# Alternating the halves of TensorE's array in four places of a one-core hybrid decoder step

## The chip, the cores and the metric

One core of a Trainium2 chip runs the whole program in one launch. The metric is the device time of one execution in microseconds (us). The kernel before was run three times: 764.14, 760.05 and 762.81 us, median 762.81.

## The reference

304 rows of 1024 numbers (16 learned rows and 256 prompt rows, and 8 sample sequences of 4 rows) go through one layer:

```
p = rmsnorm(x) @ w_in                       # columns for 4 GLA heads and for 8 RWKV-7 heads
GLA:   lg = log_sigmoid(gl @ gate_w2 + b)/16; chunked attention with decay; states
RWKV:  w, a, g by low-rank matmuls; S = S*w - (S kk)(kk a) + v k; y = S r; states
x = x + concat(norm(o_gla)*silu(gg), (norm(y)+bonus)*gate) @ w_out
x = x + moe(rmsnorm(x))                     # top 1 of 4 groups, top 2 of 8 experts, 32 SwiGLU experts
y = rmsnorm(x)
```

It returns both outputs, the GLA and RWKV states of the prompt and of the samples, and the shift rows.

## The kernel before

All of it is float32. The input projection makes 26 column tiles of 128 (tile 14 is only 32 wide where it is used here, the GLA gate columns), each as a sum over eight pieces `k` of the 1024 inputs. The rows are kept transposed, so that a matmul streams 304 columns (`T`). For most tiles the weights and the inputs are split into high and low parts (`uh`, `ul`, `xh`, `xl`) and three products are summed; for tile 14 the weights are whole (`pieces[14]`) and two products per `k` are summed, each on a group of 32 of the array's columns, with group `k % 4` (line 494 and after). The four groups are summed later by the matrix that makes `lg` (tile `ps_lg`).

The RWKV heads lie in pairs: pair `p` (0 to 3) has its two heads in partitions 0 to 63 and 64 to 127, called `q` 0 and 1. For every chunk of 64 rows of the prompt (four, and the samples as a fifth, `sct`) and every head a 64x128 matmul makes the scores (`score`, `ps_sc`, `ps_sct`); VectorE masks them into `Sc`, ScalarE and GpSimd copy the diagonal blocks into `Dm`, and a VectorE loop of 31 passes over `Lt`, the transposed `Dm`, inverts all triangles at once (`job_inverse`, tiles `tmp`, `X`). Beside that loop VectorE makes the GLA operands: `mn` and `bT` from `ps_lg`, `qT` and `kT` from the projection. `job_level` makes the six levels of GLA's decayed scores (`E`, `F`, `ps_lev`) into `AT`; `job_gla_out(q)` makes `ps_o`, `ps_omps_o` (the norm's sums) and `oG`. `job_chain` runs the five RWKV chunks one after the other (`ps_G`, `GV`, `UV`, `ps_Y`, `YT`, `ps_S`, `state`). `job_rwkv_samples` makes the eight sample states of a pair with two 128x64 matmuls of 512 columns (`ps_fs`), `job_rwkv_state` the prompt's state (`ps_fp`, 16 small matmuls). Then come the output projection (`job_oproj`, `ps_op`, 16 groups), the router, and 32 experts whose weights SyncE loads into rooms of 512 KB, or halves of 256 KB, as these come free.

Nobody writes the order of the instructions by hand. Each `job_...` is a generator that hands its operations to `Flow` (all are recorded through line 356), and `Flow` picks the next one by a price per operation, a due time (`RANK`) and its own model of what is ready. So an edit in one job can move the work of others on every engine. `bank(name, least)` takes a PSUM bank; `least` is the number that must be free.

Of the kernel before, what the change touches and what calls it, by code (L numbers as in the profile page):

```python
# [361 lines left out]
def tile_step(ctx: ExitStack, tc: tile.TileContext, io):  # L362
# [127 lines left out]
    def job_project(tiles):  # L490
        for j in tiles:
            o = yield from bank(f"ps_in{j}", 2 if j < 14 else 1)
            for k in range(KT):
                yield from after(f"x{k}", f"u{j}_{k // 4}")
                if j == 14:

                    g = 32 * (k % 4)
                    for i, x in enumerate((xh, xl)):
                        PE.matmul(o[g:g + 32, :T], pieces[14][:, k * P:k * P + 32], x[:, k, :].bitcast(F32),
                                  start=(k < 4 and i == 0), stop=(k >= 4 and i == 1))  # L500
                else:
                    kk, (hi, lo) = slice(k % 4 * P, k % 4 * P + P), units[j, k // 4]
                    for i, (w, x) in enumerate(((hi, xh), (hi, xl), (lo, xh))):
                        PE.matmul(o[:, :T], w[:, kk], x[:, k, :], start=(k + i == 0), stop=(k == KT - 1 and i == 2))
                if k % 4 == 3:
                    mark(f"p{j}_{k // 4}")
                yield
# [210 lines left out]
    def job_scores():  # L718

        for p in range(4):  # L720
# [6 lines left out]
            Sc, Dm = late["Sc"], late["Dm"]  # L727
            for q in range(2):
                o = yield from bank(f"ps_sc{p}{q}")
                for c in range(4):  # L730
                    score(o[:, c * P:(c + 1) * P], p, q, c)
                V.tensor_tensor(Sc[q][:, 0:4, p, :], o.rearrange("p (c t) -> p c t", c=4),
                                sm.unsqueeze(1).to_broadcast([P, 4, P]), ALU.mult)
                flow.release(o)
# [5 lines left out]
        for q in range(2):  # L740
            o = yield from bank(f"ps_sct{q}")
            for p in range(4):
                score(o[:, p * P:(p + 1) * P], p, q, 4)
            late[f"sct{q}"] = o
# [295 lines left out]
    def job_rwkv_samples():  # L1040
# [23 lines left out]
        for p in range(4):  # L1064
            mb = t5((6, 1)[p % 2], f"UVb{p}", [P, 2, NS, 64])
            ob = yield from bank(f"ps_fs{p}", 2)
            for q in range(2):
                r = halves(q)[0]
                V.tensor_tensor(mb[:, q], us[q][:, 64 * p:64 * p + 64].unsqueeze(1).to_broadcast([P, NS, 64]),
                                seg[:, 1:9].unsqueeze(2).to_broadcast([P, NS, 64]), ALU.mult)  # L1070
                PE.matmul(ob[r, :], BKt[:, q, p, :], mb[:, q].rearrange("p b i -> p (b i)"), start=True, stop=True)
# [10 lines left out]
    def job_rwkv_state():  # L1082
# [7 lines left out]
        for p in range(4):  # L1090
            for q in range(2):
                r = halves(q)[0]
                PE.matmul(o[r, 64 * p:64 * p + 64], BKt[:, q, p, :], m[q][:, 64 * p:64 * p + 64], start=True, stop=False)
                PE.matmul(o[r, 64 * p:64 * p + 64], ident[r, 64 * q:64 * q + 64], state[r, p, :], start=False, stop=True)
# [1381 lines left out]
```

## Time and profile before

| | us |
|---|---|
| median of three runs | 762.81 |
| the profiled execution | 768.22 |
| span of its profile | 766.4 |
| mixer with its projections, to the output projection's start | 241.0 |
| output projection and router, to the first experts' start | 241 to 297 |
| experts and end | 297 to 766 |

The profiled execution took 5.41 us more than the median. A row of the timeline is the start and the length in us, the engine, the line, and the operation with what it writes and reads; for TensorE the numbers before the tile's size are the rows and columns of the array that it uses, and the profile has two records for one float32 matmul (`x8` is four matmuls). A bracket at the end is the idle time before it and what ended it. In a window's row each engine has its busy time and its records; the three numbers at the end are the granted TensorE clock as a share of 2.4 GHz, the DMA engines' busy share and GB/s.

### The profile page before, as it was taken

What the parts mean: (1) busy time and instruction counts of PE and PEld (TensorE: products, weight loads), DVE (VectorE), ACT (ScalarE), POOL (GpSimd) and SP (SyncE); (2) the same over time, 40 slices, a digit from 0 to 9 for tenths busy, and PEclk for the clock granted to TensorE, in tenths of its full rate; (3) what the DMA queues carried; (4) which work ended last, traced back from release to release, by engine and by line L of the source; (5) the groups of instructions that cost most, each with busy time, mean ns of one, the idle gap of its engine ahead of it and who ended that gap; (6) DMA issues with size and microseconds to landing.
All of it is one profiled execution on the core that took longest, in us unless ns stands there. A gap on an engine that the chain in (4) does not pass through costs nothing.

```text
span 766.4 us, 12595 instructions
## 1 busy us (share of the span) xinstructions
PE 689.2 (90%) x4610; PEld 353.0 (46%) x4610; DVE 306.1 (40%) x619; ACT 212.4 (28%) x525; POOL 138.2 (18%) x211
## 2 busy tenths in 40 slices
PE   6989997989998989999899999999989988988893
PEld 6878677878656975442223424323222221211131
DVE  6688479874576759521022312201111111101023
ACT  6887462554224431221011201111011010000003
POOL 3277325584352100400000000000010000000000
PEclk9989789889998987999999999999999999999998
DMA  8421115114267794999999999999999999999971
GB/s 308 139 83 56 56 50 200 57 57 170 99 242 239 265 328 173 410 416 415 418 418 417 418 419 418 419 416 416 419 415 415 418 417 414 415 410 414 414 297 69
DMA packets 66581, 230.63 MB, mean 301 GB/s; under 512 B 7920, under 2 KB 8944, under 8 KB 66000
## 3 DMA queue, kind: packets, MB, share of 16 engines
q1 hardware_dynamic: 65936, 229.45, 76.2%
q8 instruction: 38, 0.62, 0.3%
q10 hardware_dynamic: 576, 0.31, 0.2%
q14 instruction: 31, 0.25, 0.1%
HBM read 226.06 MB, written 3.67 MB: 300 GB/s over the span
## 4 chain that ended last, share of the span: by engine, by line


## 5 line engine op out<-in xcount | busy, mean ns | idle before, releaser
L356 PE MATMUL ps_in<-xh,uh 128*128 128x304 f32 x160 | 53.5, 335 | 6.6 <-ACT uh L356 6.6
L356 PE MATMUL ps_in<-xh,ul 128*128 128x304 f32 x160 | 53.8, 336 | 0.0
L356 PE MATMUL ps_in<-xl,uh 128*128 128x304 f32 x160 | 53.1, 332 | 0.0
L356 ACT ACTIVATE room_y<-ps_y,sw 128x512 fp32r<-128x512 f32 x18 | 11.7, 685 | 144.0 <-PE ps_sc L356 81.6
L356 DVE TENSOR_TENSOR room_AT<-room_AT,ps_sc 128x512 f32<-128x512 f32 x8 | 5.5, 687 | 110.7 <-PE ps_sc L356 110.7
L356 POOL TENSOR_TENSOR room_xl<-cst,prm 128x512 f32<-128x512 f32 x2 | 2.0, 1042 | 246.3 <-PE ps_y L356 246.3
L356 POOL TENSOR_TENSOR ul<-win,uh 128x512 fp32r<-128x512 f32 x28 | 37.2, 1331 | 32.5 <-ACT uh L356 28.8
L356 DVE TENSOR_TENSOR room_xg<-room_xg,ps_sc 48x512 f32<-48x512 f32 x16 | 10.6, 674 | 81.0 <-PE ps_sc L356 81.0
L356 PE MATMUL ps_xg<-oh,hl 128*128 128x256 f32 (+5 forms) x192 | 41.8, 345 | 0.9 <-DVE oh L356 0.9
L356 PEld LDWEIGHTS ps_in<-xh,uh 128*128 128x128 f32 x160 | 33.4, 209 | 8.4 <-ACT uh L356 6.6
L356 PEld LDWEIGHTS ps_xg<-oh,hl 128*128 128x128 f32 (+1 forms) x192 | 29.7, 198 | 16.5 <-issue 9.1
L356 PEld LDWEIGHTS ps_in<-xl,uh 128*128 128x128 f32 x160 | 33.4, 209 | 1.5 <-issue 1.0
L356 PEld LDWEIGHTS ps_in<-xh,ul 128*128 128x128 f32 x160 | 33.2, 207 | 1.4 <-issue 0.6
L356 PE MATMUL ps_h_w<-room_w,room_w 128*32 128x512 f32 (+1 forms) x104 | 28.6, 600 | 2.3 <-DMA room_w<-in_w 2.3
L356 ACT CAST ohT<-ps_ot 128x304 fp32r<-128x304 f32 x9 | 3.7, 413 | 95.1 <-PE ps_ot L356 95.0
L356 PE MATMUL ps_sc<-room_y,ohT 128*128 128x512 f32 (+1 forms) x96 | 28.0, 413 | 0.0
L356 ACT CAST uh<-win 128x512 fp32r<-128x512 f32 x40 | 24.4, 614 | 11.8 <-PE ps_in L356 11.6
L356 PE MATMUL ps_h_w<-Sc,room_w 128*64 128x512 f32 (+1 forms) x56 | 24.4, 602 | 0.3 <-DMA Sc<-in_w 0.2
L356 DVE SCALAR_TENSOR_TENSOR room_y<-ps_y,sw,room_y 128x512 fp32r<-128x512 f32 x18 | 12.9, 739 | 29.5 <-ACT room_y L356 29.3
L356 PE MATMUL ps_in<-xh,u 128*128 128x304 f32 x96 | 22.5, 313 | 0.6 <-DVE rx L356 0.6
L356 PEld LDWEIGHTS ps_sc<-room_y,ohT 128*128 128x128 f32 (+1 forms) x96 | 14.1, 166 | 17.3 <-issue 12.5
L356 PE MATMUL ps_h_w<-room_w,BKa 128*32 128x512 f32 x52 | 18.5, 603 | 1.5 <-DMA room_w<-in_w 1.5
(734 smaller groups left out, 1634.8 us busy)
## 6 DMA issues: line engine op xcount, KB each, us to landing
room_w<-in_w SPq DMA_DIRECT2D x99, 512.0 KB, 9.9
Sc<-in_w SPq DMA_DIRECT2D x53, 512.0 KB, 9.8
room_win<-in_w SPq DMA_DIRECT2D x48, 512.0 KB, 9.9
room_o<-in_w SPq DMA_DIRECT2D x31, 512.0 KB, 10.0
room_xh<-in_w SPq DMA_DIRECT2D x30, 512.0 KB, 9.9
UV<-in_w SPq DMA_DIRECT2D x29, 512.0 KB, 9.9
win<-in_win SPq DMA_DIRECT2D x27, 512.0 KB, 3.2
room_xl<-in_w SPq DMA_DIRECT2D x26, 512.0 KB, 10.0
```

The source lines that it names most:

```text
L356: lambda: method(*args, **kw)))
```

## The change

Four edits. The gate columns are issued eight at a time, when `k` is 3 and 7: four column groups with `xh`, then the four with `xl`. The scores of a pair take both banks first and alternate between `q` 0 and 1; both masks follow; the samples' scores alternate as well. The sample states make both masked operands on VectorE first and then issue both matmuls. The prompt state issues its eight `BKa` products first and then its eight products with the identity (`cst`); the accumulation starts with the first and stops with the last.

```diff
@@ -494,10 +494,10 @@
                 yield from after(f"x{k}", f"u{j}_{k // 4}")
                 if j == 14:
 
-                    g = 32 * (k % 4)
-                    for i, x in enumerate((xh, xl)):
-                        PE.matmul(o[g:g + 32, :T], pieces[14][:, k * P:k * P + 32], x[:, k, :].bitcast(F32),
-                                  start=(k < 4 and i == 0), stop=(k >= 4 and i == 1))
+                    for kk, x in [(kk, x) for x in (xh, xl) for kk in range(k - 3, k + 1)] if k % 4 == 3 else []:
+                        g = 32 * (kk % 4)
+                        PE.matmul(o[g:g + 32, :T], pieces[14][:, kk * P:kk * P + 32], x[:, kk, :].bitcast(F32),
+                                  start=(kk < 4 and x is xh), stop=(kk >= 4 and x is xl))
                 else:
                     kk, (hi, lo) = slice(k % 4 * P, k % 4 * P + P), units[j, k // 4]
                     for i, (w, x) in enumerate(((hi, xh), (hi, xl), (lo, xh))):
@@ -725,23 +725,25 @@
                 flow.give(late["Dm"])
                 G.memset(late["Dm"], 0.0)
             Sc, Dm = late["Sc"], late["Dm"]
+
+            os_ = [(yield from bank(f"ps_sc{p}0", 2)), (yield from bank(f"ps_sc{p}1"))]
+            for c in range(4):
+                for q in range(2):
+                    score(os_[q][:, c * P:(c + 1) * P], p, q, c)
             for q in range(2):
-                o = yield from bank(f"ps_sc{p}{q}")
-                for c in range(4):
-                    score(o[:, c * P:(c + 1) * P], p, q, c)
-                V.tensor_tensor(Sc[q][:, 0:4, p, :], o.rearrange("p (c t) -> p c t", c=4),
+                V.tensor_tensor(Sc[q][:, 0:4, p, :], os_[q].rearrange("p (c t) -> p c t", c=4),
                                 sm.unsqueeze(1).to_broadcast([P, 4, P]), ALU.mult)
-                flow.release(o)
+                flow.release(os_[q])
                 yield
             for q in range(2):
                 for h in range(2):
                     r = slice(64 * q + 32 * h, 64 * q + 32 * h + 32)
                     S.copy(Dm[r, :, p:16:4], Sc[q][r, 0:4, p, 32 * h:32 * h + 32].rearrange("p c t -> p t c"))
         for q in range(2):
-            o = yield from bank(f"ps_sct{q}")
-            for p in range(4):
-                score(o[:, p * P:(p + 1) * P], p, q, 4)
-            late[f"sct{q}"] = o
+            late[f"sct{q}"] = yield from bank(f"ps_sct{q}", 2 - q)
+        for p in range(4):
+            for q in range(2):
+                score(late[f"sct{q}"][:, p * P:(p + 1) * P], p, q, 4)
         yield
         for q in range(2):
             V.tensor_tensor(Sc[q][:, 4], late[f"sct{q}"].rearrange("p (x t) -> p x t", x=4),
@@ -1065,10 +1067,10 @@
             mb = t5((6, 1)[p % 2], f"UVb{p}", [P, 2, NS, 64])
             ob = yield from bank(f"ps_fs{p}", 2)
             for q in range(2):
-                r = halves(q)[0]
                 V.tensor_tensor(mb[:, q], us[q][:, 64 * p:64 * p + 64].unsqueeze(1).to_broadcast([P, NS, 64]),
                                 seg[:, 1:9].unsqueeze(2).to_broadcast([P, NS, 64]), ALU.mult)
-                PE.matmul(ob[r, :], BKt[:, q, p, :], mb[:, q].rearrange("p b i -> p (b i)"), start=True, stop=True)
+            for q in range(2):
+                PE.matmul(ob[halves(q)[0], :], BKt[:, q, p, :], mb[:, q].rearrange("p b i -> p (b i)"), start=True, stop=True)
             yield
             V.tensor_tensor(srw[:, p], ob.rearrange("p (b i) -> p b i", b=NS), srw[:, p], ALU.add)
             G.tensor_tensor(srw[:, p], srw[:, p], WLs[:, p, :].unsqueeze(2).to_broadcast([P, NS, 64]), ALU.mult)
@@ -1089,9 +1091,12 @@
             V.tensor_scalar(pairs(m[q][:, 0:256]), UV[:, q], seg[:, 0:1], None, op0=ALU.mult)
         for p in range(4):
             for q in range(2):
+                PE.matmul(o[halves(q)[0], 64 * p:64 * p + 64], BKt[:, q, p, :], m[q][:, 64 * p:64 * p + 64],
+                          start=(p == 0), stop=False)
+        for p in range(4):
+            for q in range(2):
                 r = halves(q)[0]
-                PE.matmul(o[r, 64 * p:64 * p + 64], BKt[:, q, p, :], m[q][:, 64 * p:64 * p + 64], start=True, stop=False)
-                PE.matmul(o[r, 64 * p:64 * p + 64], ident[r, 64 * q:64 * q + 64], state[r, p, :], start=False, stop=True)
+                PE.matmul(o[r, 64 * p:64 * p + 64], ident[r, 64 * q:64 * q + 64], state[r, p, :], start=False, stop=(p == 3))
         mark("uvs")
         yield
         fp = yield from t1("fp")
```

How the instructions move, at three places.

TensorE, scores of the last pair (`ps_sc30`, `ps_sc31`) and the gate columns (`ps_in14`), before:

```order
L356 MATMUL ps_in14_1018<-xl_108,win14_739 32x304
L356 MATMUL ps_sc30_1033<-AR_115,BK_116 128x128 x4
L356 MATMUL ps_b3_1032<-rx3_685,bl3_929 128x304
L356 MATMUL ps_in14_1018<-xh_107,win14_739 32x304
L356 MATMUL ps_sc31_1043<-AR_115,BK_116 128x128 x2
L356 MATMUL ps_g3_1047<-g2_740,lw_95 128x304
L356 MATMUL ps_sc31_1043<-AR_115,BK_116 128x128 x2
L356 MATMUL ps_in14_1018<-xl_108,win14_739 32x304
L356 MATMUL ps_in14_1018<-xh_107,win14_739 32x304
L356 MATMUL ps_in14_1018<-xl_108,win14_739 32x304
L356 MATMUL ps_in14_1018<-xh_107,win14_739 32x304
L356 MATMUL ps_in14_1018<-xl_108,win14_739 32x304
```

and with the change, from the first gate column on:

```order
L356 MATMUL ps_in14_1017<-xh_107,win14_736 32x304 x4
L356 MATMUL ps_in14_1017<-xl_108,win14_736 32x304 x4
L356 MATMUL ps_sc30_1036<-AR_115,BK_116 128x128
L356 MATMUL ps_sc31_1037<-AR_115,BK_116 128x128
L356 MATMUL ps_sc30_1036<-AR_115,BK_116 128x128
L356 MATMUL ps_sc31_1037<-AR_115,BK_116 128x128
L356 MATMUL ps_sc30_1036<-AR_115,BK_116 128x128
L356 MATMUL ps_sc31_1037<-AR_115,BK_116 128x128
L356 MATMUL ps_sc30_1036<-AR_115,BK_116 128x128
L356 MATMUL ps_sc31_1037<-AR_115,BK_116 128x128
L356 MATMUL ps_in14_1017<-xh_107,win14_736 32x304
L356 MATMUL ps_b3_1035<-rx3_681,bl3_829 128x304
```

The eight scores of a pair are now neighbours that alternate, and half the gate columns precede them; behind `ps_b3` and `ps_g3` stand now `xh` x2, `xh` and `xl` x3, the eight `ps_sct` in turns, one `xl`, and then 24 matmuls of `ps_in15` with `ps_lg0` behind the eighth.

VectorE, from the samples' first masked scores to the loop's first pass, before:

```order
L356 TENSOR_TENSOR Sc0_610<-ps_sct0_1056,cst_79 128x512
L356 TENSOR_TENSOR Sc1_611<-ps_sct1_1057,cst_79 128x512
L356 TENSOR_TENSOR glT_1083<-ps_in14_1018,rstdB_223 128x304
L356 STREAM_TRANSPOSE Lt_1093<-Dm_612 128x1024
L356 TENSOR_SCALAR mn0_1102<-ps_lg0_1084,prm_78 128x304
L356 TENSOR_TENSOR tmp_1095<-Lt_1093,X_1094 128x31
L356 TENSOR_TENSOR mn0_1102<-mn0_1102,ab0_1101 128x304
L356 TENSOR_TENSOR X_1094<-X_1094,tmp_1095 128x31
```

and with the change:

```order
L356 TENSOR_TENSOR Sc0_610<-ps_sct0_1051,cst_79 128x512
L356 TENSOR_TENSOR glT_1080<-ps_in14_1017,rstdB_223 128x304
L356 TENSOR_TENSOR Sc1_611<-ps_sct1_1052,cst_79 128x512
L356 TENSOR_SCALAR mn0_1096<-ps_lg0_1081,prm_78 128x304
L356 SCALAR_TENSOR_TENSOR qT_120<-ps_in15_1078,rstdB_223 128x304
L356 TENSOR_TENSOR mn0_1096<-mn0_1096,ab0_1095 128x304
L356 SCALAR_TENSOR_TENSOR bT_122<-nsg_101,mn0_1096 128x304
L356 STREAM_TRANSPOSE Lt_1143<-Dm_612 128x1024
L356 TENSOR_SCALAR mn1_1157<-ps_lg1_1126,prm_78 128x304
L356 TENSOR_TENSOR mn1_1157<-mn1_1157,ab1_1156 128x304
L356 SCALAR_TENSOR_TENSOR bT_122<-nsg_101,mn1_1157 128x304
L356 TENSOR_TENSOR tmp_1145<-Lt_1143,X_1144 128x31
```

Both gate chains (`mn`, `bT`) and one `qT` stand now ahead of the loop; before, the second chain and both `qT` were inside it. The second `kT` stands now three passes earlier in the loop.

TensorE, the end of the mixer, before:

```order
L356 MATMUL ps_mt_2932<-YT_1790,bones64_114 128x192
L356 MATMUL ps_fp_2936<-UVp0_2937,BKa_1096 64x64
L356 MATMUL ps_fp_2936<-state3_2823,cst_79 64x64
L356 MATMUL ps_fp_2936<-UVp1_2938,BKa_1096 64x64
L356 MATMUL ps_fp_2936<-state3_2823,cst_79 64x64
L356 MATMUL ps_fp_2936<-UVp0_2937,BKa_1096 64x64
L356 MATMUL ps_fp_2936<-state3_2823,cst_79 64x64
L356 MATMUL ps_fp_2936<-UVp1_2938,BKa_1096 64x64
L356 MATMUL ps_op0_2961<-oG_2461,wout_uh0_2606 128x304 x2
```

and with the change:

```order
L356 MATMUL ps_fp_2891<-UVp1_2893,BKa_1146 64x64
L356 MATMUL ps_fp_2891<-UVp0_2892,BKa_1146 64x64
L356 MATMUL ps_fp_2891<-UVp1_2893,BKa_1146 64x64
L356 MATMUL ps_fp_2891<-state3_2778,cst_79 64x64 x4
L356 MATMUL ps_m2_2883<-ysq2_2899,bones64_114 128x256
L356 MATMUL ps_fp_2891<-state3_2778,cst_79 64x64 x4
L356 MATMUL ps_omps_o1_2709_2944<-osq_2710,onesd_133 128x512
L356 MATMUL ps_m3_2885<-ysq3_2940,bones64_114 128x256
L356 MATMUL ps_vart_2955<-ysqt_2954,bones64_114 128x192
L356 MATMUL ps_op0_2989<-oG_2345,wout_uh0_2716 128x304 x2
```

All of `ps_fp`, two sums `ps_m` and the norm of the second half of GLA's heads (`ps_omps_o1`) stand now directly ahead of `ps_op0`; before, seven `ps_fp` stood there, nine came between groups of `ps_op`, and that norm was further up, in the midst of the last chunk. On VectorE 25 instructions stand now between the last chunk's `YT` and the last `oG`; before there were five. One GLA level (40 `ps_lev`, with `E` and `F`) has moved from ahead of the chain into its third chunk. The two `ps_fs` of a pair are still parted, before by `ps_G` or nothing, now by `ps_os`, `ps_G`, `ps_S` and `ps_G`. On SyncE 48 of the experts' weight loads that were 24 of 128x1024 are now 128x512.

## Rows read from the trace of the kernel before

**Rows 1.** The page: span and busy time of each engine.
```profile
span 766.4 us, 12595 instructions
...
PE 689.2 (90%) x4610; PEld 353.0 (46%) x4610; DVE 306.1 (40%) x619; ACT 212.4 (28%) x525; POOL 138.2 (18%) x211
```

**Rows 2.** Windows of the span: from and to, length, busy time and records of PE, PEld, DVE, ACT, POOL; granted clock, DMA share, GB/s.
```profile
86.20:88.20 2.00, 2.00 (x7) 1.06 (x6) 0.55 (x1) 0.41 (x1) 0.83 (x1) 0.59 0.48 182
88.20:98.00 9.80, 9.80 (x41) 5.36 (x40) 2.08 (x3) 3.44 (x8) 1.50 (x3) 0.50 0.00 0
98.00:100.00 2.00, 2.00 (x8) 1.52 (x7) 1.62 (x2) 0.00 (x0) 1.66 (x3) 0.50 0.42 123
120.00:140.00 20.00, 16.10 (x272) 15.41 (x269) 19.21 (x48) 3.80 (x8) 9.01 (x12) 0.83 0.29 109
186.00:241.00 55.00, 51.43 (x531) 34.18 (x530) 38.78 (x67) 18.24 (x44) 23.91 (x20) 0.93 0.60 206
...
276.00:279.00 3.00, 3.00 (x27) 2.73 (x25) 0.90 (x3) 1.99 (x4) 0.00 (x0) 1.00 0.95 317
286.00:297.00 11.00, 7.78 (x38) 4.03 (x37) 10.48 (x34) 0.95 (x3) 1.33 (x4) 0.50 0.19 66
300.00:740.00 440.00, 405.14 (x1870) 124.56 (x1863) 82.50 (x145) 56.20 (x149) 11.17 (x11) 1.00 1.02 415
```

**Rows 3.** Timeline of TensorE, last scores and gate columns.
```profile
75.96 1.16 PE L356 MATMUL ps_sc<-AR,BK 64*128 64x128 f32 x8
77.04 0.41 PE L356 MATMUL ps_in<-xh,ul 128*128 128x304 f32 x1
...
82.09 0.73 PE L356 MATMUL ps_in<-xh,win 128*32 128x304 f32 x6
...
83.26 1.16 PE L356 MATMUL ps_sc<-AR,BK 64*128 64x128 f32 x8
85.50 0.78 PE L356 MATMUL ps_b<-rx,bl 128*128 128x304 f32 x2 [1.08 <-POOL rx L356]
...
87.07 1.22 PE L356 MATMUL ps_sc<-AR,BK 64*128 64x128 f32 x4
88.22 1.38 PE L356 MATMUL ps_g<-g,lw 128*128 128x304 f32 x2
...
90.68 0.71 PE L356 MATMUL ps_in<-xl,win 128*32 128x304 f32 x1
90.69 0.74 PE L356 MATMUL ps_in<-xh,win 128*32 128x304 f32 x3
...
92.87 3.09 PE L356 MATMUL ps_sct<-AR,BK 64*128 64x128 f32 x16
...
98.06 0.62 PE L356 MATMUL ps_in<-xh,uh 128*128 128x304 f32 x1
```

**Rows 4.** Timeline of TensorE, two matmuls on different row halves of the array.
```profile
29.22 0.52 PE L356 MATMUL ps_w<-wa,lw 64*128 64x304 f32 x1
29.23 0.52 PE L356 MATMUL ps_a<-wa,lw 64*128 64x304 f32 x1
```

**Rows 5.** Timeline of VectorE: `Lt`, the loop's second pass, and the second `kT`.
```profile
98.56 1.23 DVE L356 STREAM_TRANSPOSE Lt<-Dm 128x1024 f32<-128x1024 f32 x1
...
104.42 0.20 DVE L356 TENSOR_TENSOR tmp<-Lt,X 128x60 f32<-128x60 f32 x1
...
133.62 0.47 DVE L356 SCALAR_TENSOR_TENSOR kT<-ps_in,rstdB 128x304 f32<-128x304 f32 x1
```

**Rows 6.** Timeline of TensorE: the second group of the first GLA level.
```profile
134.14 0.61 PE L356 MATMUL ps_lev<-qT,kT 64*32 64x32 f32 x40 [3.23 <-DVE kT L356]
```

**Rows 7.** Timeline of TensorE: the third pair's sample states.
```profile
196.33 1.07 PE L356 MATMUL ps_fs<-UVb,BKa 128*64 128x512 f32 x2
...
197.59 1.07 PE L356 MATMUL ps_fs<-UVb,BKa 128*64 128x512 f32 x2
198.59 0.68 PE L356 MATMUL ps_Y<-AR,state 64*64 64x64 f32 x16
```

**Rows 8.** Timeline of VectorE at the end of the chain.
```profile
236.77 0.41 DVE L356 TENSOR_TENSOR YT<-ps_Y,SPt 128x256 f32<-128x256 f32 x1
...
239.04 0.68 DVE L356 TENSOR_TENSOR oG<-osq,oG 128x512 fp32r<-128x512 f32 x1
```

**Rows 9.** Timeline of TensorE: norm of the second half of GLA's heads, and the first group of the output projection.
```profile
227.87 1.13 PE L356 MATMUL ps_omps_o<-osq,onesd 128*128 128x512 f32 x2
...
241.00 0.88 PE L356 MATMUL ps_op<-oG,wout_uh 128*128 128x304 f32 x2
```

**Rows 10.** Timeline of ScalarE on the same norm.
```profile
229.76 0.63 ACT L356 ACTIVATE osq<-osq 128x512 f32<-128x512 f32 x1 [1.77 <-DVE osq L356]
...
236.73 0.60 ACT L356 CAST oG<-osq 128x512 fp32r<-128x512 f32 x1
```

**Rows 11.** Timeline of GpSimd on the same norm.
```profile
235.12 1.45 POOL L356 TENSOR_TENSOR osq<-osq,sg 128x512 f32<-128x512 f32 x1 [0.46 <-DVE osq L356]
```

**Rows 12.** Timeline of TensorE: a group of `ps_fp` between groups of `ps_op`.
```profile
246.03 0.33 PE L356 MATMUL ps_fp<-state,cst 64*64 64x64 f32 x2
...
246.79 0.55 PE L356 MATMUL ps_op<-oG,wout_uh 128*128 128x304 f32 x2
```

## Prediction

> **What bounds the kernel now.** I read the page first, then windows, then the timelines of TensorE and VectorE in the stretches that the edits touch. TensorE is busy for 90% of the span [rows 1], but two stretches differ. From 300 us on the DMA engines are full and move 415 GB/s [rows 2]: the experts take as long as their weights take to arrive, so that part only shifts when the mixer ends earlier. Ahead of it TensorE carries the path, with VectorE close behind: from 120 to 140 VectorE is busy for 19.21 of 20 us and TensorE for 16.10 [rows 2], and TensorE waits there 3.23 us for `kT` [rows 6]. From 286 to 297 the DMA engines are mostly idle (0.19) [rows 2], so the shift of the mixer's end should reach the experts whole. The edits save TensorE time; the question is which of it arrives at 241.00, where the output projection starts [rows 9].
>
> **Scores and gate columns.** Four scores of one half take 77.04 - 75.96 = 1.08 us at full clock, 0.27 each; at half clock two take 88.22 - 87.07 = 1.15, 0.575 each [rows 3]. Two matmuls on different row halves start 0.01 us apart [rows 4], so I take an alternating pair at the price of one. Gate columns of different groups run together already: `xl` and three `xh` start within 0.01 us of each other although the order parts them [rows 3]. Six of them take 83.26 - 82.09 = 1.17 us at full clock and 92.87 - 90.68 = 2.19 at half [rows 3], two slots each, 0.58 and 1.1 a slot. So rotating them gains only where they are cut into short runs: seven slots become six.
>
> Up to the last pair I count nothing: `ps_b` at 85.50 waits for GpSimd's `rx` [rows 3], which comes from VectorE's chain and not from TensorE. (Bounds: 0 to 2 us, what two of those 1.08 us would give if that chain came earlier by it.) From 85.50 the changed order has `ps_b`, a gate slot, `ps_g`, a gate slot, four pairs of `ps_sct`, a gate slot. At half clock that is 0.7 + 1.1 + 1.3 + 1.1 + 4 x 0.575 + 1.1 = 7.6 us; at full clock 0.7 + 0.58 + 0.7 + 0.58 + 4 x 0.27 + 0.58 = 4.2. Before it is 98.06 - 85.50 = 12.6 [rows 3]. The gain is 5.0 or 8.4. The clock was 0.59 right behind the wait of 1.08 us and 0.50 up to 100 [rows 2, 3]; TensorE reaches that wait earlier now and waits longer, so I take half clock, 5.0: the gate columns are done at 93.1.
>
> The Trainium skill, "TensorE: Matmul & The Clock Gate", Part 3, says that a weight load overlaps running matmuls only where the row group differs. By it column groups of the same rows would not run together, rotating them would save no slot, and the sum below would be 1.1 us higher, 763.4. The trace does not agree: four start within 0.01 us [rows 3].
>
> **What VectorE makes of it.** TensorE next needs `kT`, and there the changed order costs something back. `qT` now stands ahead of `Lt` and waits for 24 projection matmuls behind the gate columns; at half clock eight of them take 2.0 us [rows 2], so `qT` runs at 93.1 + 6.0 = 99.1. Behind it come a gate chain, `Lt`, the second chain and the first pass. From `Lt` to the second pass, with one chain, took 104.42 - 98.56 = 5.9 us [rows 5]; with about 1.3 for the rest of the other chain the second pass starts at 106.3, later than before. But between it and the second `kT` are now missing the second chain (2.2), a `qT` (0.47) and three passes (2.3): 5.0 of the 133.62 - 104.42 = 29.2 us [rows 5]. The second `kT` comes at 130.5, 3.1 earlier; at full clock (gate columns at 89.7, `qT` 3.4 behind) 9 earlier. I take **-3.5**: the clock was back at full at 100 before, and may be back for some of those matmuls. TensorE would wait some 5 us for `kT` instead of 3.23.
>
> **Sample states.** Each pair of `ps_fs` is still parted by a matmul of another shape. Such a parted pair took 198.59 - 196.33 = 2.26 us, the second starting 1.26 behind the first [rows 7]: no overlap. So **0**. If the two overlapped, four times 1.0 would go: -4 at the other end.
>
> **The end of the mixer.** Before, the last `oG` ran 2.27 us behind `YT` with five instructions between, 0.38 for each instruction [rows 8], and `ps_op` 4.23 behind `YT` [rows 8, 9]. Now 25 stand between: 26 x 0.38 = 9.9 us, or, at VectorE's mean of this stretch, 38.78 / 67 = 0.58 [rows 2], 15. The second norm's own chain also lies there: its matmul 1.13, VectorE 0.7, two steps on ScalarE of 0.63, VectorE 0.7, GpSimd 1.45, ScalarE 0.60, `oG` 0.68 [rows 8 to 11], 6.5 in all, and its matmul cannot start much before 4.5 behind `YT`, since the sums ahead of it wait for VectorE's `yc`. So 11 at least. I take 13 and the last `oG` of 0.68: 13.5 against 4.2, +9.3. On the other side that norm (1.13) and five sums `ps_m` of about half its size leave the stretch ahead of `YT`, and some `ps_o`: 1.13 + 5 x 0.55 less the 0.61 of the level that comes in [rows 6, 9], -3.3 and a little more. Net **+5.5**, bounds +1 (the projection starts on the first half's `oG` and hides the rest) and +11.5 (15 + 0.68 - 4.2, and `YT` no earlier). `ps_fp` costs nothing there, since TensorE waits anyway. The moved level is paid ahead of the chain or in it: 0.
>
> **Output projection.** Three groups of three `ps_fp`, 246.79 - 246.03 = 0.76 us each [rows 12], no longer stand between groups of `ps_op`: -2.3, and `ps_vart` -0.2. **-2.5**, bounds -1 and -3.
>
> **Weights.** 24 loads of 512 KB become 48 of 256 KB. Where halves and whole loads were mixed, 276 to 279, the rate was 317 GB/s against 415 [rows 2]. For 12.6 MB that is 30 us or 40; but that window also waits for free rooms. I take **+0.5**, bounds 0 and +6.
>
> **Sum.** -3.5 + 0 + 5.5 - 2.5 + 0.5 = 0.0. With a little for the earlier scores, -0.5: the profiled execution of 768.2 becomes 767.7, and on the scale of the median, which is 5.4 lower, 762.8 becomes **762.3**. A measurement of this kernel can tell about 0.5%, 3.8 us, from no change.
>
> **Rivals.** *The front's gain arrives.* The wait at `ps_b` is short enough for the clock to stay, the gate columns end at 89.7 and `kT` comes 9 us earlier: -9 + 5.5 - 2.5 + 0.5 = -5.5, 757.3; with the projection starting on the first half of `oG` another 4 less, 753. For it: the 14 us at half clock, 86.2 to 100 [rows 2], follow the only wait in this stretch. Against it: the wait is still there.
>
> *The tail takes more.* VectorE's 25 instructions behind `YT` go at the mean of 0.58, and TensorE's earlier work doesn't bring `YT` forward: +11.5 instead of +5.5, in all -3.5 + 11.5 - 2.5 + 0.5 = +6, **768.8**, slower. It decides from the point where the last `oG` lies 10.5 us or more later behind `YT` than before (-3.5 - 2.5 + 0.5 + 10 = +4.5). For it: ScalarE, GpSimd and TensorE lie in that chain in turn, each in its own order. Against: in the same stretch TensorE was busy for 51.43 of 55 us [rows 2], so taking work from ahead of `YT` should bring it forward.
>
> *The change does not do what it says.* Pairs of scores run one behind the other after all. Then the front gains almost nothing: 0 + 5.5 - 2.5 + 0.5 = +3.5, 766.3. The pair of `ps_w` and `ps_a` speaks against it [rows 4].
>
> **Chances.** Forecast 0.43, of which 0.34 lie within 0.5%, 0.06 below and 0.03 above; the front's gain 0.30; the longer tail 0.17; no overlap 0.10, half of it within 0.5%. So faster 0.36, same 0.39, slower 0.25. The forecast's own range is 758 to 767; with the rivals' prices the range that leaves out 2 in 10 is 754 to 769.
>
> **What would show it.** Right: eight scores of a pair in about 1.1 us at full clock; gate columns done some 5 us earlier; TensorE waiting around 5 us for the second `kT`; `ps_fs` as before; 6 to 10 us of idle TensorE between `ps_fp` and `ps_op`; the projection shorter by 2 us or more. The forecast is wrong if TensorE does not wait at `kT`, if `ps_op` follows `YT` by less than 8 or more than 17 us, or if the experts from 300 us on take over 2 us longer than before.

## The result and the profile after

The changed kernel took 756.46 us (median; 752.84 to 765.28), the kernel before 762.57 beside it (760.05 to 772.00): a ratio of 0.990 [0.985, 0.994], 6.1 us or 1.0% faster. The forecast was 762.3 and no change, with a range of 754 to 769. The range holds the time; it lies nearest to the first rival's 757.3.

The profiled execution of the changed kernel is its longest, 765.28, because the clock of TensorE stayed at half for a while under the first experts (below); the ratios leave such executions out, so medians and ratios need not agree.

The page after, span and engines [rows 1]:

```profile
span 763.5 us, 12698 instructions
...
PE 680.0 (89%) x4610; PEld 342.4 (45%) x4610; DVE 305.7 (40%) x619; ACT 212.1 (28%) x525; POOL 133.2 (17%) x211
```

Windows after [rows 2], same columns:

```profile
88.20:98.00 9.80, 9.80 (x72) 6.86 (x71) 4.91 (x9) 6.51 (x14) 5.20 (x6) 1.00 0.33 106
...
120.00:140.00 20.00, 14.99 (x177) 14.13 (x176) 19.55 (x47) 7.93 (x20) 11.99 (x14) 0.83 0.29 102
186.00:241.00 55.00, 46.09 (x510) 31.51 (x510) 41.23 (x77) 20.43 (x49) 18.56 (x21) 0.94 0.72 259
270.00:300.00 30.00, 24.56 (x109) 13.57 (x108) 26.39 (x78) 2.63 (x8) 1.54 (x5) 0.50 0.60 224
300.00:740.00 440.00, 403.76 (x1826) 124.45 (x1826) 72.70 (x126) 55.41 (x147) 10.46 (x11) 0.98 1.01 407
```

The clock (third number from the end) from 88 to 98 is 1.00 where it was 0.50, and 0.50 from 270 to 300.

TensorE after, last scores and gate columns [rows 3]:

```profile
85.22 1.16 PE L356 MATMUL ps_sc<-AR,BK 64*128 64x128 f32 x14 [0.76 <-POOL BK L356]
86.30 0.70 PE L356 MATMUL ps_in<-xh,win 128*32 128x304 f32 x2
87.63 0.78 PE L356 MATMUL ps_b<-rx,bl 128*128 128x304 f32 x2 [0.63 <-POOL rx L356]
...
90.33 1.16 PE L356 MATMUL ps_sct<-AR,BK 64*128 64x128 f32 x16
91.43 0.70 PE L356 MATMUL ps_in<-xl,win 128*32 128x304 f32 x2
```

Eight scores take 1.1 us, the price of four before. The last `ps_b` waits 0.63 and not, as forecast, longer than 1.08; a new wait of 0.76 for `BK` stands ahead of it, so the two together are longer (1.39). It starts 2.1 later than in [rows 3], and the gate columns end 4.5 behind it, at 92.1.

VectorE after [rows 5, 8], and TensorE's wait for the second `kT` [rows 6]:

```profile
98.94 1.21 DVE L356 STREAM_TRANSPOSE Lt<-Dm 128x1024 f32<-128x1024 f32 x1
...
125.11 0.47 DVE L356 SCALAR_TENSOR_TENSOR kT<-ps_in,rstdB 128x304 f32<-128x304 f32 x1
...
217.51 0.42 DVE L356 TENSOR_TENSOR YT<-ps_Y,SPt 128x256 f32<-128x256 f32 x1
...
232.26 0.69 DVE L356 TENSOR_TENSOR oG<-osq,oG 128x512 fp32r<-128x512 f32 x1
```

```profile
125.63 0.67 PE L356 MATMUL ps_lev<-qT,kT 64*32 64x32 f32 x40 [4.32 <-DVE kT L356]
```

The second `kT` comes 8.5 earlier than in the first profile of before, and the last `oG` starts 14.75 behind the last `YT` in place of 2.27. TensorE between them [rows 9, 12]:

```profile
220.27 0.69 PE L356 MATMUL ps_fp<-UVp,BKa 128*64 128x64 f32 x16
220.89 0.45 PE L356 MATMUL ps_fp<-state,cst 64*64 64x64 f32 x8
221.26 0.70 PE L356 MATMUL ps_m<-ysq,bones 128*128 128x256 f32 x2
221.89 0.45 PE L356 MATMUL ps_fp<-state,cst 64*64 64x64 f32 x8
224.24 1.12 PE L356 MATMUL ps_omps_o<-osq,onesd 128*128 128x512 f32 x2 [1.90 <-ACT osq L356]
...
226.43 0.57 PE L356 MATMUL ps_op<-oG,wout_uh 128*128 128x304 f32 x2
226.83 0.30 PE L356 MATMUL ps_op<-oG,wout_ul 128*128 128x304 f32 x1
230.58 0.62 PE L356 MATMUL ps_op<-oG,wout_uh 128*128 128x304 f32 x1 [3.45 <-ACT oG L356]
233.00 0.62 PE L356 MATMUL ps_op<-oG,wout_uh 128*128 128x304 f32 x1 [1.80 <-DVE oG L356]
```

The projection starts on the first half's `oG` and then waits 3.45 and 1.80 us for the second half's: 7.5 us of waiting in all, 2.2 of them ahead of the projection, between the last `YT` and the first `xr` (VectorE's addition of the projection's first result, at 235.43).

### The profile page after: what moved, and what is told of

Read it like the earlier page. It is cut to its first block, busy times and chain, and to the rows that moved or that the text cites. A ratio compares the mean times of both kernels' runs of the same rounds, so it can differ in the third digit from the quotient of the medians.

```text
span 763.5 us, 12698 instructions
## 1 busy us (share of the span) xinstructions
PE 680.0 (89%) x4610; PEld 342.4 (45%) x4610; DVE 305.7 (40%) x619; ACT 212.1 (28%) x525; POOL 133.2 (17%) x211
## 4 chain that ended last, share of the span: by engine, by line
## 5 line engine op out<-in xcount | busy, mean ns | idle before, releaser
L356 DVE TENSOR_TENSOR room_w<-room_w,ps_sc 128x512 f32<-128x512 f32 (+1 forms) x48 | 31.2, 680 | 203.8 <-PE ps_sc L356 196.1
L356 PE MATMUL ps_in<-xh,uh 128*128 128x304 f32 x160 | 51.6, 322 | 6.7 <-ACT uh L356 6.7
L356 PE MATMUL ps_in<-xh,ul 128*128 128x304 f32 x160 | 51.5, 322 | 0.0
L356 PE MATMUL ps_xg<-oh,hl 128*128 128x256 f32 (+5 forms) x192 | 45.5, 369 | 0.9 <-DVE oh L356 0.9
L356 POOL TENSOR_TENSOR ul<-win,uh 128x512 fp32r<-128x512 f32 x28 | 36.8, 1316 | 29.5 <-ACT uh L356 25.8
L356 PEld LDWEIGHTS ps_xg<-oh,hl 128*128 128x128 f32 (+1 forms) x192 | 32.9, 220 | 18.5 <-issue 8.2
L356 PE MATMUL ps_h_w<-Sc,room_w 128*32 128x512 f32 (+1 forms) x88 | 35.3, 602 | 1.2 <-DMA Sc<-in_w 1.1
L356 PE MATMUL ps_h_w<-room_w,room_w 128*32 128x512 f32 (+1 forms) x64 | 26.6, 601 | 2.0 <-DMA room_w<-in_w 2.0
L356 PE MATMUL ps_h_w<-room_win,room_w 128*32 128x512 f32 (+1 forms) x76 | 25.7, 600 | 1.1 <-DMA room_win<-in_w 1.1
L356 PE MATMUL ps_h_w<-UV,room_w 128*64 128x512 f32 (+1 forms) x48 | 23.6, 600 | 0.8 <-DMA UV<-in_w 0.7
L356 PE MATMUL ps_h_w<-BKa,room_w 128*32 128x512 f32 (+1 forms) x44 | 22.0, 601 | 1.3 <-DMA BKa<-in_w 1.3
```

Source lines behind the costliest of these rows:

```text
L356: lambda: method(*args, **kw)))
```

## The experiments

Starts from the timelines, in us; `changed` is the changed kernel's profile above, "experts" is from the first expert's first matmul to the end of the span. The intervals are of the ratio to the kernel before on the same chip.

| kernel | last ps_b | first ps_U | last YT | first xr | logits end | first expert | experts | ratio |
|---|---|---|---|---|---|---|---|---|
| before | 85.50 | 186.74 | 236.77 | 244.13 | 283.77 | 293.40 | 473.0 | 1 |
| before_again | 87.37 | 181.55 | 230.04 | 236.41 | 276.53 | 286.16 | 473.4 | |
| changed | 87.63 | 172.86 | 217.51 | 235.43 | 272.21 | 281.84 | 481.7 | 0.990 [0.985, 0.994] |
| again | 87.36 | 175.97 | 220.62 | 238.55 | 274.17 | 283.80 | 471.3 | 0.990 [0.984, 0.996] |
| changed_b | 91.76 | 178.34 | 222.98 | 240.89 | 278.90 | 288.52 | 482.1 | 0.989 [0.983, 0.996] |
| serial_scores | 94.48 | 179.96 | 224.61 | 242.53 | 279.90 | 289.54 | 471.3 | 0.995 [0.990, 1.000] |
| paired_gates | 87.17 | 176.51 | 221.16 | 239.08 | 275.15 | 284.77 | 470.8 | 0.989 [0.976, 1.002] |
| states_undone | 91.77 | 178.31 | 222.95 | 243.74 | 281.23 | 290.85 | 471.2 | 0.994 [0.990, 0.999] |
| all_undone | 92.40 | 179.86 | 224.51 | 245.49 | 283.33 | 292.96 | 483.0 | 0.997 [0.992, 1.002] |
| out_early | 87.55 | 173.40 | 223.07 | 232.49 | 270.98 | 280.62 | 471.4 | 0.994 [0.990, 0.999] |
| out_first | 90.60 | 175.57 | 234.55 | 236.12 | 283.32 | 292.94 | 471.8 | 1.009 [1.006, 1.013] |
| warm_router | 87.03 | 173.47 | 218.12 | 236.04 | 272.74 | 281.48 | 471.9 | 0.989 [0.985, 0.993] |
| warm_logits | 87.42 | 176.05 | 220.69 | 238.61 | 276.60 | 285.20 | 471.6 | 0.990 [0.985, 0.995] |
| tail_and_warm | 92.19 | 178.57 | 223.22 | 239.45 | 274.94 | 283.69 | 472.2 | 0.990 [0.985, 0.994] |

**The two kernels again.** No edit in `again`, `changed_b` and `before_again`.

> The changed kernel once more, beside the kernel before. In its first profile the first expert matmul stood 11.6 us earlier than before (281.84 against 293.40 us), but the execution was only 2.9 us shorter, and the window 300 to 320 had a granted clock of 0.72 and 233 GB/s where before had 1.00 and 389. Theory 1: the mixer's gain of 11 to 12 us holds in every execution, and what differs is how long the clock stays at half at the start of the experts; a profile of another execution then shows the first expert matmul at 281 to 283 us, and a span shorter by as much as the clock comes back sooner: ratio 0.985 to 0.993, single executions down to 752. Theory 2: the gain itself varies with the clock in the mixer (the gate columns at half clock in one execution, at full in another); then the first expert matmul comes at 286 to 290 in a profile where 86 to 98 us is at half clock.

> The changed kernel once more, for comparison on one chip with the two that follow: ratio to before 0.988 to 0.992, first expert matmul at 281.5 to 284, last YT to first xr 17.9, last ps_b done by 87.5.

> A second profile of the kernel before, to see whether the half clock of its profiled stretch from 86 to 100 us belongs to the kernel or to that one execution. If it belongs to the kernel: granted clock near 0.50 again from 86 to 98, gate columns done at about 98, first expert matmul at 293 +-1. If it belongs to the execution: clock above 0.9 there, gate columns done near 93 (the eight scores 1.7 instead of 3.1, the sixteen gate matmuls at half their price), kT some 5 earlier, first expert matmul near 287 to 289; then the 10 to 11.6 us by which the profiled first expert came earlier after the change are only 4 to 7 of the change itself.

The ratio repeats (0.990, 0.989). The milestones do not repeat as closely: the first expert starts at 283.80 in `again`, but at 288.52 in `changed_b`, where 281.5 to 284 was expected, because the clock fell between 72 and 84 (0.72) and the last `ps_b` came 4.4 later. The second profile of before, window and timeline of TensorE:

```profile
84.00:100.00 16.00, 14.89 (x150) 9.66 (x151) 7.02 (x14) 8.69 (x22) 7.31 (x12) 1.00 0.20 67
```

```profile
85.11 1.16 PE L356 MATMUL ps_sc<-AR,BK 64*128 64x128 f32 x8
87.37 0.78 PE L356 MATMUL ps_b<-rx,bl 128*128 128x304 f32 x2 [1.11 <-POOL rx L356]
...
91.86 1.71 PE L356 MATMUL ps_sct<-AR,BK 64*128 64x128 f32 x16
...
94.04 0.68 PE L356 MATMUL ps_in<-xl,win 128*32 128x304 f32 x2
```

The same wait (1.11 against 1.08) was not followed by half clock this time. So the 14 us at half clock in [rows 2, 3] are no fixed part of the kernel: here the gate columns end 7.35 behind `ps_b` and not 12.6. With this and other differences of the clock the first expert comes 7.2 earlier than in the first profile; of the 11.6 us by which it came earlier after the change, as the first two profiles have it, 4.3 are left.

**Scores by halves in turn.** All engines keep the changed order; the eight scores of a pair alone go back to four of `q` 0, then four of `q` 1 (`emit` permutes the last calls recorded).

```diff
+            emit(8, [0, 2, 4, 6, 1, 3, 5, 7])
...
+        emit(8, [0, 2, 4, 6, 1, 3, 5, 7])
```

> The changed kernel with every instruction of every engine where it is, but in each set of eight scores the four of the first half go first and then the four of the second half (masks stay behind the eight). Theory 1 (pairs on different row halves run together, and that is where the gain comes from): the last pair's eight scores take 1.6 to 2.2 us at full clock instead of 1.2, those of the samples 1.5 to 2.2 instead of 1.1, and the time rises by 2 us if the clock stays and by 5 to 8 if it falls there as it did before: ratio to the kernel before 0.993 to 1.000. Theory 2 (the gain is the new order of everything else): ratio within 0.3% of that of the changed kernel run beside it.

```profile
64.62 1.71 PE L356 MATMUL ps_sc<-AR,BK 64*128 64x128 f32 x16
...
97.18 1.71 PE L356 MATMUL ps_sct<-AR,BK 64*128 64x128 f32 x16
```

Eight in a row by halves take 1.71, as the samples' eight do in `before_again`; alternating they take 1.16 in the changed kernel. So the order itself is worth 0.55 us per eight at full clock; only against two fours with other work between (1.16 each, [rows 3]) is it about 1.1. The last `ps_b` comes 2.7 later than in `changed_b`, where the clock fell at the same place, from 72 on. The time lies between: 0.995, an interval that overlaps that of `again`. The two kernels ran beside each other, so their times can also be compared directly: the executions that the ratios use have means of 761.3 and 757.5, a difference of 3.8 +- 2.5 us (95% interval, worked out here from the single times). So this order is worth something in the time, clear of the noise.

**Gate columns.** The two products of a column group are neighbours again; only TensorE's rows differ.

```diff
-for kk, x in [(kk, x) for x in (xh, xl) for kk in range(k - 3, k + 1)]
+for kk, x in [(kk, x) for kk in range(k - 3, k + 1) for x in (xh, xl)]
```

> The changed kernel with every other instruction where it is, but in each set of eight gate column products the two of one column group follow each other, as in the kernel before. Theory 1 (the array runs column groups together whatever the order of neighbours, since before the change four started within 0.01 us although the order parted them): the first eight take 1.1 to 1.3 us as with rotation (1.16), and the time is within 0.2% of the changed kernel. Theory 2 (rotation is needed): the first eight take 2 us or more and the time rises by 1 to 3 us.

First eight of `again`, then of `paired_gates`:

```profile
82.53 0.72 PE L356 MATMUL ps_in<-xh,win 128*32 128x304 f32 x8
83.06 0.69 PE L356 MATMUL ps_in<-xl,win 128*32 128x304 f32 x8
```

```profile
82.31 0.74 PE L356 MATMUL ps_in<-xh,win 128*32 128x304 f32 x8
82.84 0.71 PE L356 MATMUL ps_in<-xl,win 128*32 128x304 f32 x8
```

The second four start 0.53 behind the first in both. TensorE brings the column groups together whichever way the eight are written, so the rotation gains nothing here; the ratio, 0.989, has too wide an interval to say more. The Trainium skill, "TensorE: Matmul & The Clock Gate", Part 3, says that weight loads overlap running matmuls only between row groups, but the same part also lists a gain of 2.38 times for three matmuls on different column tiles. The prediction took the first statement alone and made of it that column groups would not run together; here all eight use all 128 rows and four still run together, as the second says.

**Prompt states.** The sixteen matmuls of `ps_fp` go back to product and identity in turns.

```diff
-                          start=(p == 0), stop=False)
+                          start=True, stop=False)
...
-                PE.matmul(o[r, ...], ident[r, ...], state[r, p, :], start=False, stop=(p == 3))
+                PE.matmul(o[r, ...], ident[r, ...], state[r, p, :], start=False, stop=True)
+        emit(16, [i // 2 + 8 * (i % 2) for i in range(16)])
```

> The changed kernel with the prompt states' sixteen matmuls back in the order of before (product and state by turns, 64x64 alternating with 64x64 of the other kind); nothing else moves on any engine. Theory 1 (in the tail TensorE's rows stand in front of the means that VectorE needs for oG): sixteen take 4.1 (16 starts, 0.257 apart) in place of 2.0, last YT to first xr 20 to 21 in place of 17.9, first expert 2 to 3 later, ratio to before about 0.993. Theory 2 (the tail has 7.5 us of TensorE's waiting, which takes the two up): 17.9 as before, no difference.

Its profile and that of `changed_b` happen to agree to 0.1 us up to the last `YT`, which makes them a clean pair. TensorE in `changed_b`, then in `states_undone`:

```profile
225.74 0.69 PE L356 MATMUL ps_fp<-UVp,BKa 128*64 128x64 f32 x16
...
226.73 0.70 PE L356 MATMUL ps_m<-ysq,bones 128*128 128x256 f32 x2
...
229.70 1.12 PE L356 MATMUL ps_omps_o<-osq,onesd 128*128 128x512 f32 x2 [1.89 <-ACT osq L356]
```

```profile
225.71 0.33 PE L356 MATMUL ps_fp<-UVp,BKa 128*64 128x64 f32 x2
225.97 0.32 PE L356 MATMUL ps_fp<-state,cst 64*64 64x64 f32 x2
...
228.79 0.70 PE L356 MATMUL ps_m<-ysq,bones 128*128 128x256 f32 x2
...
231.76 1.84 PE L356 MATMUL ps_omps_o<-osq,onesd 128*128 128x512 f32 x2 [1.25 <-ACT osq L356]
```

By turns, each starts 0.257 behind the last. `ps_m`, on which the norm waits, starts 2.06 later, `ps_omps_o` 2.06, the first `xr` 2.9 (the clock was lower there: 1.84 for 1.12), the first expert 2.3. Theory 1 holds: TensorE's 7.5 us of waiting come behind these rows and can't take them up. In the time, 0.994 against 0.989 is 3.7 us, with intervals that overlap; compared directly, the two kernels' times differ by 4.5 +- 4.3 us, just clear of the noise.

**All three orders undone.** The three edits above together, in the changed order otherwise.

```diff
+            emit(8, [0, 2, 4, 6, 1, 3, 5, 7])
...
-for kk, x in [(kk, x) for x in (xh, xl) for kk in range(k - 3, k + 1)]
+for kk, x in [(kk, x) for kk in range(k - 3, k + 1) for x in (xh, xl)]
...
+        emit(16, [i // 2 + 8 * (i % 2) for i in range(16)])
```

> The changed kernel with the scores, the gate columns and the prompt state in the order of the kernel before inside their own sets, and all else, on every engine, where the change put it. Theory 1 (overlap on the array makes the gain): time within 0.4% of the kernel before, ratio 0.996 to 1.004. Theory 2 (the new order makes it): ratio within 0.3% of the changed kernel, about 0.990. Between: the sum of what the two runs beside it show, plus less than 0.5 us for the prompt state, since TensorE waits behind it anyway.

The ratio is 0.997 [0.992, 1.002]: the moved work by itself, with both `ps_fs` masks first, cannot be told from the kernel before. Against `again`, which ran beside it, the times are 5.8 +- 2.9 us longer (means 763.3 and 757.5, worked out as above), so what gain there is goes when these orders go. The profiles agree where the clock does: `changed_b` also fell to 0.72 between 72 and 84, and its first expert starts at 288.52, 4.4 us ahead of the 292.96 here.

**The tail.** Only `'gla_out'` in `RANK` moves; at 2.4 fourteen of the 25 VectorE instructions between the last `YT` and the last `oG` leave that stretch, at 1.0 all of the `oG` stand ahead of `YT`.

```diff
-'gla_out': 4.49
+'gla_out': 2.4
```

> The changed kernel with one number of the table moved: 'gla_out' 4.49 to 2.4, so that 14 DVE instructions that stood between YT and the last oG are issued behind the oG, and TensorE's order is the same up to the end of the chain. Theory 1 (the tail is paced by VectorE's order): the last oG starts about 8 us behind the last YT instead of 14.75, the first xr about 10 to 12 behind it instead of 17.9, the first expert 5 to 7 earlier, ratio to before about 0.980 to 0.984. Theory 2 (the work moved behind the oG is wanted just as soon, by the output projection or by the weights of the third state): YT to xr falls, but xr to the end of the router logits grows by as much from 36.8, and the time stays at 756 to 757.

```diff
-'gla_out': 4.49
+'gla_out': 1.0
```

> The same number at 1.0: the oG pieces are done ahead of the last YT. Theory 1: the last oG no longer paces the first ps_op at all, which starts 1 to 3 us behind the last YT; but the chain in front of YT carries the pieces, U to YT 46 to 50 instead of 44.65; first expert 3 to 8 earlier than in the changed kernel. Theory 2: as for the run before, no gain: 756 or more, as the pieces now delay the chain by as much as the tail gains.

VectorE in `out_early`:

```profile
223.07 0.42 DVE L356 TENSOR_TENSOR YT<-ps_Y,SPt 128x256 f32<-128x256 f32 x1
...
228.90 1.09 DVE L356 TENSOR_TENSOR oG<-osq,oG 128x512 fp32r<-128x512 f32 x1
...
232.49 0.48 DVE L356 TENSOR_TENSOR xr<-ps_op,xr 128x304 f32<-128x304 f32 x1 [1.95 <-PE ps_op L356]
```

From `YT` to `xr` the tail shrinks from 17.9 to 9.4, as theory 1 said. But `ps_U` to `YT` grows from 44.65 to 49.7, which neither theory had, and `xr` to the logits' end from 36.8 to 38.5: 8.5 - 5.0 - 1.7 = 1.8 are left of it in the profile and nothing in the time (0.994). With `oG` first, `ps_U` to `YT` takes 59.0 and the kernel is slower than before. So the long tail is mostly work moved out of the chain, not time lost.

**The clock of the first experts.** In every profile the clock falls to 0.50 in the router's logits. In most it is back 14 to 17 us later; in `changed`, `changed_b` and `all_undone` it stayed at half for 41 to 48 us, to 311, 321 and 326, and the experts took 481.7 to 483.0 in place of 470.8 to 473.4. Two kernels put unused matmuls there.

```diff
         mark("raw")
+        ow = yield from bank("ps_warm")
+        for _ in range(12):
+            PE.matmul(ow, hl[0][0][:, 0:P], hl[0][0][:, 0:512], start=True, stop=True)
```

> The changed kernel with twelve further matmuls (128x512, their result unused) in TensorE's wait between the router's logits and the ranks, which is 4.55 us long. Theory 1 (the clock of the first experts falls because TensorE stood still there): clock of 1.00 from the first expert on in the profile, first expert to the end of the span 470 to 471.5 in place of the 481.7 of the changed kernel's first profile, and the runs lie closer together, near 753. Theory 2 (the clock at that place does not depend on this wait): first expert to end still 471 in some executions and 481 in others, the median within 2 us of the changed kernel's, or 1 to 2 more if the twelve take longer than the wait.

```diff
+            if j == 5:
+                ow = yield from bank("ps_warm")
+            if j >= 5:
+                PE.matmul(ow[:, 0:256], xr(j)[:, 0:P], xr(j)[:, 0:256], start=True, stop=True)
             yield
...
         mark("raw")
+        for _ in range(10):
+            PE.matmul(ow, hl[0][0][:, 0:P], hl[0][0][:, 0:512], start=True, stop=True)
```

> The changed kernel with three unused 128x256 f32 matmuls among the last three of the router's eight groups of logits, and ten unused 128x512 behind the last of them, in the wait for the choice of experts. In the run with twelve behind the logits alone the clock had fallen before the first of the twelve was issued, during the logits' narrow matmuls, and came back when they ended. Theory 1 (the narrow matmuls are what the clock falls on): with wide ones among them the clock is 1.00 through the logits and at the first expert, which then starts 1 to 3 us earlier relative to the end of the logits' last matmul (8.7 to 9.6 so far), and the runs' spread above 760 goes away; median 752 to 755. Theory 2 (the fall at that place belongs to what came before the logits, and the wide ones change nothing): clock 0.50 from about 271 on as before, the end of the logits 1.3 later by the three, time as the changed kernel's or 1 more.

Windows of `warm_router`, then of `warm_logits`:

```profile
272.00:278.00 6.00, 6.00 (x17) 4.41 (x16) 4.45 (x25) 0.42 (x2) 0.50 (x2) 0.50 0.92 341
278.00:282.00 4.00, 3.13 (x26) 2.31 (x28) 3.37 (x8) 0.73 (x2) 0.00 (x0) 0.93 0.01 5
282.00:286.00 4.00, 4.00 (x23) 1.49 (x15) 3.96 (x10) 0.00 (x0) 0.35 (x1) 0.60 0.03 10
286.00:300.00 14.00, 14.00 (x112) 7.22 (x115) 13.45 (x36) 4.28 (x15) 0.71 (x2) 1.00 0.98 383
```

```profile
264.00:274.00 10.00, 10.00 (x80) 9.28 (x78) 3.27 (x9) 3.35 (x9) 0.00 (x0) 1.00 0.92 306
274.00:282.00 8.00, 8.00 (x32) 6.34 (x31) 4.44 (x25) 0.42 (x2) 0.49 (x2) 0.57 0.71 270
```

Neither first theory holds as put: the clock had fallen before the twelve began, and with wide matmuls among the logits it fell all the same. In both it came back behind them, fell once more and was at 1.00 from 288 at the latest. What they may do is bring it back sooner. Of 24 executions with such matmuls (these two and the next kernel) 2 took over 763 us, of 25 of the changed kernel 8. That is suggestive at most: the batches differ, `out_early`, which has no such matmuls, had 1 of 12, and the ratios are the same (0.989, 0.990).

**Both together.** The twelve, and later due times for the sample tokens' norm and for `fp`, meant to put them behind the last `oG` on VectorE. In the profile the norm goes there, all but its first operation; `fp` stays ahead.

```diff
-'tail_norms': 0.44, ... 'rwkv_state': 0.69
+'tail_norms': 8, ... 'rwkv_state': 6
...
+        for _ in range(12):
+            PE.matmul(ow, hl[0][0][:, 0:P], hl[0][0][:, 0:512], start=True, stop=True)
```

> The changed kernel with two numbers of the table moved, 'tail_norms' 0.44 to 8 and 'rwkv_state' 0.69 to 6, so that the sample tokens' own norm (yct, oT) and the prompt states' fp stand behind the last oG on VectorE instead of ahead of it, TensorE's tail being the same but for one ps_m that moves ahead of ps_fp; and with the twelve unused 128x512 matmuls behind the router's logits. Theory 1 (VectorE's rows between YT and the last oG set the tail's end): last oG 12 to 13 behind the last YT in place of 14.75, last YT to first xr 15.5 to 16.5 in place of 17.9, the end of the logits 1.5 to 2.5 earlier relative to YT, and with the twelve the median at 752 to 754.5, ratio 0.984 to 0.988. Theory 2 (the sample tokens' norm is wanted just as soon, by the oTs that the projection's second half takes): the first xr is earlier but the logits end no earlier, 54.7 behind the last YT as in the changed kernel, and the ratio stays at 0.989 to 0.991.

The profile does what theory 1 said: `oG` 11.8 behind `YT`, `xr` 16.2, logits' end 51.7 where `warm_router` had 54.6. The time does not: 756.34, ratio 0.990, like the changed kernel's. In this one profile the clock fell between 72 and 84, and the last `ps_b` was 5.2 later than in `warm_router`, more than the tail's 2.9; whether that is so in the other executions isn't shown. No version was shown to beat the changed kernel.

## Where the prediction was right and where it was off, step by step

The range held the time, and the main signs came as forecast: eight scores in 1.1 us, in the first profile a wait of 4.3 for the second `kT` (some 5 said), the first `ps_op` 8.9 behind `YT` (8 to 17 said). The forecast of no change did not hold: working from one profile, the sum compared a half-clock front before with a half-clock front after. Full against full (`before_again`, then `again` and `changed`) the stages come out so:

| stage | predicted | again | changed |
|---|---|---|---|
| start to first ps_U | -3.5 | -5.6 | -8.7 |
| first ps_U to first xr | +5.5 | +7.7 | +7.7 |
| first xr to logits' end | -2.5 | -4.5 | -3.3 |
| experts | +0.5 | -2.1 | (clock) |
| sum | 0.0 | -4.5 | |

-4.5 is what the two executions differ by (761.45 and 756.90); the medians differ by 6.1.

**The step that failed first is the front's clock**: "TensorE reaches that wait earlier now and waits longer, so I take half clock". Its `ps_b` starts no earlier (87.4 to 91.8 in the three profiles against 85.5 and 87.4) and waits 0.63, with the wait for `BK` ahead of it. In all twelve profiles of the changed order and its variants the clock from 88 to 100 was 1.00. The full-clock sum given there, 4.2, is near what was measured, 4.5. Why half clock followed the wait in one execution of the kernel before and in none of the others is not shown. Against this profile of before, `kT` came 8.5 earlier, the rival's 9; but the rival's baseline had the same half clock, and against `before_again` `kT` gains 3.2 in `changed`, 5.1 in `again` and nothing in `changed_b` (VectorE in `before_again`, against the 125.11 above):

```profile
128.33 0.47 DVE L356 SCALAR_TENSOR_TENSOR kT<-ps_in,rstdB 128x304 f32<-128x304 f32 x1
```

That the taken -3.5 lies so near is chance: both sides of the difference were too long. The rival's 757.3 came near by chance as well, with 9 at `kT` for these 0 to 5 and with 5.5 for the 7.7 of the mixer's end.

The rest of the front's gain lies behind `kT`, where the forecast counted 0. From `kT` to `ps_U` it took 53.2 in `before_again`, 47.8 in `changed` and 52.8 in `again` (at a mean clock of 0.97, 0.91 and 0.86). From the end of the gate columns to `ps_U` TensorE's waits fell from 9.25 to 6.56 and 5.88. But part of it is no gain: the GLA level that moved behind `ps_U` (0.94 on TensorE, some 3.5 on VectorE) is missing in this stage and is paid in the next.

"Up to the last pair I count nothing" missed a loss: with earlier scores TensorE waits more for GpSimd and VectorE (6.7 to 8.0 us from 40 to 98 in the three, against 4.0), and half clock followed either at 60 to 68 (0.79), or at 72 to 84 (0.72), which costs another 4.4 at `ps_b` (`changed_b`). In part this is a shift: from 40 to 60 the clock was 0.83 and 0.74 in the two profiles of before, 0.83 to 0.91 in the three.

**The other steps.** Pairs of scores: right, 1.1 per eight. Gate slots: right that the groups run together, and of the rotation nothing is left. Sample states: 0, as said, but not for every pair as said. Three pairs are parted as before. The third pair has only `ps_S` beside it, which uses tiles of the same shape (128 rows, 64 columns), and its two matmuls overlap (profile of the changed kernel):

```profile
183.16 1.07 PE L356 MATMUL ps_fs<-UVb,BKa 128*64 128x512 f32 x2
...
186.21 0.73 PE L356 MATMUL ps_S<-UV,BKa 128*64 128x64 f32 x16
186.72 1.08 PE L356 MATMUL ps_fs<-UVb,BKa 128*64 128x512 f32 x4
```

The kernel before did the same for that pair (`before_again`; [rows 7] show the second pair, not the third):

```profile
196.82 0.64 PE L356 MATMUL ps_fs<-UVb,BKa 128*64 128x512 f32 x1
...
197.00 1.02 PE L356 MATMUL ps_fs<-UVb,BKa 128*64 128x512 f32 x3
```

So one pair of four overlaps in either kernel, and the edit gains nothing there. The end of the mixer: the chain's part right (-3.8, said -3.3), the last `oG` at 14.75, said 13, so net +7.7 for +5.5 (against the first profile +5.2). "`ps_fp` costs nothing there, since TensorE waits anyway" was wrong in its reason: by turns it would cost 2 to 3 us, and the edit's grouping is what keeps it small. Projection: right in kind, 1 to 2 us more than said, though the stage goes on to the logits' end and holds stretches of either clock. Weights: wrong in sign, experts 0.8 to 2.6 us shorter in the profiles where the clock came back; why was not tried.

Not settled: how often the kernel before has its half-clock stretch at 86 to 100 (one profile of two), and so how much of the 6.1 us is instructions and how much is the clock that they leave.

## What to carry to other kernels

Profile the kernel before twice before costing a stretch at half clock: the same wait of 1.1 us was followed by it in one execution and not in the next, and two profiles of one kernel differed by 7 us at the first expert. Idle time hides only what stands behind it on its engine: here 2.06 us of matmuls ahead of the norm's sums moved them by 2.06, with over 5 us of waiting still to come. And work moved out of a chain into its tail shows up as a longer tail; undo it before calling the tail a loss.

## What was not expected of the hardware

Eight matmuls in two runs of four on the two row halves take 1.71 us, less than two fours apart (2.3) and more than alternating (1.16): neighbouring runs overlap in part without any edit. Eight matmuls on four column groups take the same in either order (the second four start 0.53 us behind the first). Small matmuls of two shapes in turns start 0.257 us apart; sorted by shape, the twelve ahead of `ps_m` took 1.0 us in place of 3.1. And TensorE's clock, once at half under the router, came back after 14 to 17 us in most profiles and after 41 to 48 in three, with experts that took some 8 to 12 us longer.
